# Fixing the order of the scan's output products: the two heads of a chunk in turn, then the products with the carried states

## The chip, the cores and the metric

The kernel runs on one core of one Trainium2 chip. The metric is the time of the whole program on the device in microseconds, lower is better. The time before the change is the median of three runs.

## What is computed

A decoder trunk of two layers on one sequence of 512 tokens, 1024 wide, all in float32. Layer 0 mixes by dilated attention, layer 1 by a Mamba-2 scan, and after each mixer stands a gated feed-forward part with a short convolution. The change lies in the scan of layer 1. Cut to that, the reference is:

```python
# 32 heads of 64, 8 groups of 4 heads, state 128, 4 chunks of 128 tokens
lmat   = jnp.exp(jnp.where(causal, seg, -jnp.inf))
cb     = jnp.einsum("bcign,bcjgn->bcijg", cm, bm)
y_diag = jnp.einsum("bcijgr,bcjgrp->bcigrp", cb[..., None] * lmat, xdt)
states = jnp.einsum("bcjgn,bcjgr,bcjgrp->bcgrpn", bm, decay, xdt)
# prev[c]: the state carried into chunk c, a recurrence over the chunks
y_off  = jnp.einsum("bcign,bcgrpn->bcigrp", cm, prev) * jnp.exp(a_cs)[..., None]
return (y_diag + y_off).reshape(b, s, h, p)
...
y = y + d_skip.astype(jnp.float32)[:, None] * xs
y = gated_group_rmsnorm(y.reshape(bsz, s, SSM_D_INNER), z, norm_w, SSM_GROUPS)
return y.astype(h.dtype) @ w_out
```

## The kernel before

Activations lie transposed, channels on the 128 partitions and 512 tokens along the free axis. Every large product is made of three products of rounded halves (high by high, low by high, high by low), each 128x128 by 128x512; all of them come from line 126 and fill one of three PSUM banks. A weight tile is loaded by SyncE's queue (line 113), rounded on ScalarE (line 117), and its low half is taken on VectorE, for the gate tiles z on GpSimd (line 118).

The scan goes through eight groups of four heads. `weave` sets the projections of the next group and products of the output matrix (tiles named wso) between the stages of `scan_group` for the present one, so that TensorE has long products to run while the small ones of the scan wait. A group has two halves x = 0 and 1 of two heads each; a half is called an output here, 16 in all, and 5.1 is group 5, x = 1. For an output:

- `by_token` turns x by tokens (px, line 648), scales it to `xdt` on VectorE (line 650) and to `xdd` on GpSimd (line 651).
- `states` makes three products `pst` (line 661), copies the first to `prev` on ScalarE (line 663), and adds the other two along the chunks on VectorE (lines 666 and 670). Chunks 1, 2 and 3 of the output need the first, second and third part of `prev`.
- `decays` loads a row of decays for each head, subtracts and takes the exponential, and multiplies by `cb` on GpSimd (line 688); the result is `lm`, one for each head.
- `outputs` is what is changed. `pf` are three products of the carried states with the C tile, 128 columns each and 128 rows of output (line 695). `py` are eight products, two heads by four chunks (line 702); each gives 64 rows of output, head 0 to the lower and head 1 to the upper 64 partitions of one bank, and so uses one half of the columns of the array. A float32 product stands in the trace as two records of TensorE: three pf are 6 records, eight py are 16. VectorE then joins py, pf, the skip term and the gate to `yt` (lines 708 to 713).

After both outputs of a group, `ss` (line 190) sums squares, `prg` (line 201) spreads the norm's factor, and VectorE and ScalarE make the two halves of y (lines 751 to 754), which the wso products read.

The order on each engine isn't the order of the code. A planner puts the instructions in order by times that it assumes, under the dependences; where a block stands under `tc.manual_schedule` for an engine, the instructions of the block keep the order of the code on that engine, and others may still come between them. An engine runs its instructions strictly in the planner's order, so an instruction that waits holds all behind it.

Of the kernel before, what the change touches and what calls it, by code (L numbers as in the profile page):

```python
# [14 lines left out]
P = 128  # L15
# [13 lines left out]
NCH = S // P  # L29
# [22 lines left out]
def trunk(ctx: ExitStack, tc: tile.TileContext, A, out):  # L52
    nc = tc.nc
    V, SC, G, T = nc.vector, nc.scalar, nc.gpsimd, nc.tensor
# [15 lines left out]
    def aux_bank(name):  # L70
        return ps.tile([P, 512], F32, tag="aux", name=name, bufs=3)

    def side_bank(name):
        return ps.tile([P, 512], F32, tag="side", name=name, bufs=2)

    def t2(name, tag, bufs, pool=k2, dtype=F32):
        return pool.tile([P, 512], dtype, tag=tag, name=name, bufs=bufs)

    def high_low(name):

        return t2(f"{name}h", "hl", 16, dtype=F32R), t2(f"{name}l", "hl", 16, dtype=F32R)
# [21 lines left out]
    def col(c):  # L103
        return par[:, c : c + 1]
# [79 lines left out]
    def inv_rms(ssum, n, r, more=None):  # L184

        p = aux_bank("ss")
        cn = r.shape[-1]
        for j in range(cn):
            js = slice(j * P, (j + 1) * P)
            T.matmul(p[:, j : j + 1], ssum[:, js], ones[:, 0:1], start=True, stop=more is None)  # L190
            if more is not None:
                T.matmul(p[:, j : j + 1], more[:, js], ones[:, 0:1], start=False, stop=True)
        ms = sm.tile([P, 4], F32, tag="ms", name="ms")
        V.tensor_scalar(ms[:, :cn], p[:, 0:cn], 1.0 / n, EPS, op0=ALU.mult, op1=ALU.add)
        G.tensor_tensor(r, ms[:, :cn], mhalf[:, :cn], op=ALU.pow)

    def along_free(r, name):

        p = aux_bank(name)
        for j in range(r.shape[-1]):  # L200
            T.matmul(  # L201
                p[:, j * P : (j + 1) * P], r[:, j : j + 1].to_broadcast([P, P]), ident,
                start=True, stop=True,
            )
        return p
# [342 lines left out]
    def b3(ap, n):  # L548

        return ap.unsqueeze(3).to_broadcast([ap.shape[0], ap.shape[1], ap.shape[2], n])  # L550
# [88 lines left out]
    def scan_group(g, d, ys):  # L639

        bt, ct, xs = d["b"], d["c"], (d["x0"], d["x1"])
        heads = [slice(4 * g + 2 * x, 4 * g + 2 * x + 2) for x in range(2)]
        xdt, xdd, prev, ee, lm = [], [], [], [], []

        def by_token(x):
            px = aux_bank("px")
            for c in range(NCH):
                T.transpose(px[:, c * P : (c + 1) * P], xs[x][:, c * P : (c + 1) * P], ident)
            t, u = t2("xdt", "xdt", 2, lp), t2("xdd", "tmp", 2, lp)
            V.tensor_tensor(v4(t), v4(px), b3(dt3[:, :, heads[x]], 64), op=ALU.mult)  # L650
            G.tensor_tensor(
                v4(u[:, 0:384], 3), v4(t[:, 0:384], 3), b3(dec3[:, 0:3, heads[x]], 64), op=ALU.mult
            )
            xdt.append(t)
            xdd.append(u)

        def states(x):
            pst = aux_bank("pst")
            for c in range(3):
                cs = slice(c * P, (c + 1) * P)  # L660
                T.matmul(pst[:, cs], btok[:, cs], xdd[x][:, cs], start=True, stop=True)
            t = t2("prev", "prev", 1, lp)
            SC.copy(t[:, 0:P], pst[:, 0:P])
            for c in range(1, 3):
                now, was = slice(c * P, (c + 1) * P), slice((c - 1) * P, c * P)
                V.tensor_tensor(
                    two(t[:, now]), two(t[:, was]),
                    cd3[:, c, heads[x]].unsqueeze(2).to_broadcast([P, 2, 64]), op=ALU.mult,
                )
                V.tensor_tensor(t[:, now], t[:, now], pst[:, now], op=ALU.add)  # L670
            prev.append(t)

        def decays(x):
            e_ = t2("ee", "ee", 2, lp)
            for hp in range(2):
                h = heads[x].start + hp
                t = t2("lm", "lm", 5, lp)
                dma(t, rows[h : h + 1, :].to_broadcast([P, S]))
                half = slice(hp * 64, (hp + 1) * 64)
                SC.activation(e_[half, P:512], t[half, P:512], AF.Exp)  # L680
                for c in range(NCH):
                    cs = slice(c * P, (c + 1) * P)
                    V.tensor_scalar(
                        t[:, cs], t[:, cs], acs[:, c * NSH + h : c * NSH + h + 1], 0.0,
                        op0=ALU.subtract, op1=ALU.min,
                    )
                SC.activation(t, t, AF.Exp)
                G.tensor_tensor(t, t, cb, op=ALU.mult)
                lm.append(t)
            ee.append(e_)  # L690

        def outputs(x):
            py, pf = side_bank("py"), side_bank("pf")
            for c in range(1, NCH):
                T.matmul(
                    pf[:, c * P : (c + 1) * P], prev[x][:, (c - 1) * P : c * P],
                    ct[:, c * P : (c + 1) * P], start=True, stop=True,
                )
            for hp in range(2):
                for c in range(NCH):  # L700
                    cs = slice(c * P, (c + 1) * P)
                    T.matmul(
                        py[hp * 64 : (hp + 1) * 64, cs],
                        xdt[x][:, c * P + hp * 64 : c * P + (hp + 1) * 64], lm[2 * x + hp][:, cs],
                        start=True, stop=True,
                    )
            yt = t2("yt", "yt", 2, lp)
            V.tensor_tensor(ee[x][:, P:512], ee[x][:, P:512], pf[:, P:512], op=ALU.mult)
            V.scalar_tensor_tensor(
                yt, xs[x], col(C_DSK + 2 * g + x), py, op0=ALU.mult, op1=ALU.add  # L710
            )
            V.tensor_tensor(yt[:, P:512], yt[:, P:512], ee[x][:, P:512], op=ALU.add)
            V.tensor_tensor(yt, yt, d[f"z{x}"], op=ALU.mult)
            sq = t2("gsq", "sq", 2)
            SC.activation(sq, yt, AF.Square)
            return yt, sq


        by_token(0)
        pb = aux_bank("pb")  # L720
        for c in range(3):
            T.transpose(pb[:, c * P : (c + 1) * P], bt[:, c * P : (c + 1) * P], ident)
        btok = t2("btok", "btok", 1, lp)
        SC.copy(btok[:, 0:384], pb[:, 0:384])
        pc = aux_bank("pc")
        for c in range(NCH):
            cs = slice(c * P, (c + 1) * P)
            T.matmul(pc[:, cs], bt[:, cs], ct[:, cs], start=True, stop=True)
        cb = t2("cb", "cb", 2, lp)
        V.tensor_tensor(  # L730
            cb.rearrange("p (c i) -> p c i", c=NCH), pc.rearrange("p (c i) -> p c i", c=NCH),
            tri.unsqueeze(1).to_broadcast([P, NCH, P]), op=ALU.mult,
        )
        yield
        decays(0)
        states(0)
        by_token(1)
        yield
        y0, sq0 = outputs(0)
        decays(1)  # L740
        states(1)
        yield
        y1, sq1 = outputs(1)
        V.tensor_tensor(sq0, sq0, sq1, op=ALU.add)
        yield
        rg = sm.tile([P, 4], F32, tag="rg", name="rg")
        inv_rms(sq0, 2 * P, rg)
        yield
        prg = along_free(rg, "prg")
        for x, y in enumerate((y0, y1)):  # L750
            V.scalar_tensor_tensor(y, y, col(C_GN + 2 * g + x), prg, op0=ALU.mult, op1=ALU.mult)
            y_h, y_l = high_low(f"y{g}{x}")
            SC.copy(y_h, y)
            V.tensor_tensor(y_l, y, y_h.bitcast(F32), op=ALU.subtract)
            ys.append((y_h, y_l))
# [181 lines left out]
```

## Time and profile before

| | |
|---|---|
| median of three runs | 1708.27 us (1706.97 to 1708.58) |
| the profiled execution, its own time | 1708.01 us |
| its span, first to last instruction | 1706.2 us |
| mean granted TensorE clock | 0.992 |
| TensorE products busy | 1675.4 us, 98% |
| VectorE, ScalarE, GpSimd busy | 64%, 40%, 28% |

The profile tells for each engine how long it was busy, how long it sat idle before an instruction, and which event ended that. Busy time of TensorE counts a product from its start to its modelled end, and neighbours overlap: two long products of 0.38 us follow at a distance of 0.22 us. So times on TensorE are read here from start to start. A full clock is 2.4 GHz and shows as 1.00, its other level 1.2 GHz as 0.50.

### The profile page before, as it was taken

Reading aid. Unit: us, or ns where it says so; the run is one execution under the profiler, and the core shown is the slowest. Engines: PE = TensorE matmul, PEld = TensorE weight load, DVE = VectorE, ACT = ScalarE, POOL = GpSimd, SP = SyncE. Lnnn points to the kernel's source line nnn. Section 1 sums busy time; section 2 is a strip of 40 time slices with the busy share of each in tenths; the row PEclk is TensorE's granted clock in tenths of the full one; section 3 lists DMA queues with packets and bytes.
Section 4 is the critical chain, followed back from the end, with each engine's and each line's share of the span. In section 5 each row is a group of like instructions: output and inputs, shape, how many; then the busy total and the mean of one; then the engine's idle time right before and its main releaser. Section 6 shows DMA issues by size and latency. Waiting matters only on the chain. (4 is left out here: it accounts for less than half of the span.)

```text
span 1706.2 us, 21506 instructions
## 1 busy us (share of the span) xinstructions
PE 1675.4 (98%) x8208; PEld 1414.4 (83%) x8208; DVE 1089.2 (64%) x1791; ACT 690.7 (40%) x1016; POOL 477.3 (28%) x312
## 2 busy tenths in 40 slices
PE   8999999999999999999999999999999999999997
PEld 6888888888888888888887888888887788888887
DVE  6366664366657746745568788787785774574565
ACT  4233332333344423423355655544562443343345
POOL 2344443144413211211242123322311321121024
PEclk9999999999999999999999999999999999999999
DMA  6222222222223223223133222232231222322324
GB/s 209 99 74 87 75 86 87 87 87 75 85 93 120 99 87 111 99 87 111 65 120 115 91 99 94 80 119 98 94 103 65 74 99 87 111 99 87 107 82 133
DMA packets 52342, 165.56 MB, mean 97 GB/s; under 512 B 5840, under 2 KB 8144, under 8 KB 52240
## 3 DMA queue, kind: packets, MB, share of 16 engines
q1 hardware_dynamic: 52240, 164.19, 28.9%
q8 instruction: 65, 1.06, 0.3%
q14 instruction: 37, 0.30, 0.1%
HBM read 162.01 MB, written 2.16 MB: 96 GB/s over the span
## 5 line engine op out<-in xcount | busy, mean ns | idle before, releaser
L126 PE MATMUL u<-xl,hi_u 128*128 128x512 f32 x704 | 271.3, 385 | 3.1 <-DVE xl L171 3.1
L126 PE MATMUL u<-xh,hi_u 128*128 128x512 f32 x704 | 271.2, 385 | 0.0
L126 PE MATMUL u<-xh,lo_u 128*128 128x512 f32 x704 | 271.0, 385 | 0.0
L517 POOL TENSOR_TENSOR au<-au,au 128x512 f32<-128x512 f32 x44 | 57.0, 1296 | 434.0 <-DVE au L497 413.3
L310 POOL TENSOR_TENSOR rotqk<-rotqk,sr 32x512 f32<-32x512 f32 x48 | 91.9, 1915 | 262.5 <-DVE rotqk L309 219.5
L497 DVE SCALAR_TENSOR_TENSOR au<-usu,par,au 128x511 f32<-128x511 f32 (+1 forms) x176 | 161.0, 919 | 6.8 <-ACT au L495 1.7
L117 ACT CAST hi_u<-raw_u 128x1024 fp32r<-128x1024 f32 x88 | 91.1, 1042 | 180.0 <-PE u L126 121.6
L126 PEld LDWEIGHTS u<-xl,hi_u 128*128 128x128 f32 x704 | 132.6, 188 | 29.8 <-DVE xl L171 4.6
L126 PEld LDWEIGHTS u<-xh,lo_u 128*128 128x128 f32 x704 | 132.5, 188 | 25.4
L126 PEld LDWEIGHTS u<-xh,hi_u 128*128 128x128 f32 x704 | 132.5, 188 | 25.3
L126 PE MATMUL qk<-xh,hi_qk 128*128 128x512 f32 x384 | 149.1, 388 | 0.0
L126 PE MATMUL qk<-xl,hi_qk 128*128 128x512 f32 x384 | 148.1, 386 | 0.0
L126 PE MATMUL qk<-xh,lo_qk 128*128 128x512 f32 x384 | 147.1, 383 | 0.0
L512 DVE TENSOR_TENSOR usu<-u,rbc 128x512 f32<-128x512 f32 x88 | 60.6, 691 | 118.1 <-PE u L126 111.6
L118 DVE TENSOR_TENSOR lo_u<-raw_u,hi_u 128x1024 fp32r<-128x1024 f32 x88 | 108.4, 1235 | 27.9 <-ACT hi_u L117 27.9
L530 DVE TENSOR_TENSOR xr<-xr,wd 128x512 f32<-128x512 f32 x40 | 27.2, 686 | 117.2 <-PE wd L126 117.2
L117 ACT CAST hi_qk<-raw_qk 128x1024 fp32r<-128x1024 f32 x48 | 50.2, 1046 | 127.9 <-PE qk L126 73.1
L117 ACT CAST hi_wd<-raw_wd 128x1024 fp32r<-128x1024 f32 (+1 forms) x56 | 52.5, 953 | 119.3 <-PE wd L126 74.7
L306 DVE TENSOR_TENSOR qk<-qk,cr 128x512 f32<-128x512 f32 x48 | 33.0, 687 | 91.0 <-PE qk L126 90.8
L182 POOL TENSOR_TENSOR ssum<-ssum,sq 128x512 f32<-128x512 f32 (+1 forms) x40 | 55.1, 1378 | 106.5 <-ACT sq L181 105.5
L126 PEld LDWEIGHTS qk<-xh,lo_qk 128*128 128x128 f32 x384 | 72.0, 188 | 13.2
L126 PEld LDWEIGHTS qk<-xh,hi_qk 128*128 128x128 f32 x384 | 72.1, 188 | 12.7
(631 smaller groups left out, 4052.0 us busy)
## 6 DMA issues: line engine op xcount, KB each, us to landing
raw_u<-in_wup SPq DMA_DIRECT2D x88, 512.0 KB, 3.2
raw_qk<-in_wqk SPq DMA_DIRECT2D x48, 512.0 KB, 3.2
raw_wd<-in_wdn SPq DMA_DIRECT2D x32, 512.0 KB, 3.2
raw_wd<-in_wdn SPq DMA_DIRECT2D x24, 384.0 KB, 2.9
raw_xs<-in_win SPq DMA_DIRECT2D x16, 512.0 KB, 3.2
raw_z<-in_win SPq DMA_DIRECT2D x16, 512.0 KB, 3.2
lm<-rows SPq DMA_DIRECT2D x32, 256.0 KB, 3.5
raw_wso<-in_wso SPq DMA_DIRECT2D x16, 512.0 KB, 3.3
```

Source lines behind the costliest of these rows:

```text
L117: SC.copy(hi[:, s], raw[:, s])
L118: low.tensor_tensor(lo[:, s], raw[:, s], hi.bitcast(F32)[:, s], op=ALU.subtract)
L126: T.matmul(in_turns(dst), w, in_turns(x), start=first, stop=last)
L182: G.tensor_tensor(ssum, ssum, sq, op=ALU.add)
L306: V.tensor_tensor(at(t), of(p), of(cr), op=ALU.mult)
L310: G.tensor_tensor(rot[R, :], rot[R, :], sr[R, :], op=ALU.mult)
L497: V.scalar_tensor_tensor(dst[:, j:], src[:, : S - j], col(c_w + taps - 1 - j), dst[:, j:], op0=ALU.mult, op1=ALU.add,)
L512: V.tensor_tensor(us, p, rbc, op=ALU.mult)
L517: G.tensor_tensor(ab[1], ab[0], ab[1], op=ALU.mult)
L530: V.tensor_tensor(xr[m], xr[m], p, op=ALU.add)
```

## The change

In `outputs`, the eight products py are put ahead of the three products pf. The heads alternate: for each chunk head 1, then head 0. The pf follow in one piece, last chunk first. The block stands under `manual_schedule` for TensorE, which keeps that order. No product is added or removed, and the other engines' work is the same.

```diff
--- before.py
+++ after.py
@@ -691,18 +691,21 @@
 
         def outputs(x):
             py, pf = side_bank("py"), side_bank("pf")
-            for c in range(1, NCH):
-                T.matmul(
-                    pf[:, c * P : (c + 1) * P], prev[x][:, (c - 1) * P : c * P],
-                    ct[:, c * P : (c + 1) * P], start=True, stop=True,
-                )
-            for hp in range(2):
+
+
+            with tc.manual_schedule(engines={mybir.EngineType.PE}):
                 for c in range(NCH):
                     cs = slice(c * P, (c + 1) * P)
+                    for hp in (1, 0):
+                        T.matmul(
+                            py[hp * 64 : (hp + 1) * 64, cs],
+                            xdt[x][:, c * P + hp * 64 : c * P + (hp + 1) * 64], lm[2 * x + hp][:, cs],
+                            start=True, stop=True,
+                        )
+                for c in reversed(range(1, NCH)):
                     T.matmul(
-                        py[hp * 64 : (hp + 1) * 64, cs],
-                        xdt[x][:, c * P + hp * 64 : c * P + (hp + 1) * 64], lm[2 * x + hp][:, cs],
-                        start=True, stop=True,
+                        pf[:, c * P : (c + 1) * P], prev[x][:, (c - 1) * P : c * P],
+                        ct[:, c * P : (c + 1) * P], start=True, stop=True,
                     )
             yt = t2("yt", "yt", 2, lp)
             V.tensor_tensor(ee[x][:, P:512], ee[x][:, P:512], pf[:, P:512], op=ALU.mult)
```

What the planner makes of it is seen on TensorE's order. In these rows a tile stands left of the arrow, what it is made from right of it; a number behind a name is that of the tile; [waits ...] names the engines waited for.

The first place is output 4.1 on TensorE, before:

```order
L126 MATMUL c_8913<-xl_97,hi_c_8908 128x4x32x4
L126 MATMUL c_8913<-xh_89,lo_c_8909 128x4x32x4
L695 MATMUL pf<-ac_8494,prev 128x128 [waits DVE_49,Activation_49]
L702 MATMUL py<-lm,xdt 64x128 [waits DVE_49]
L695 MATMUL pf<-ac_8494,prev 128x128 [waits DVE_49]
L702 MATMUL py<-lm,xdt 64x128 x6
L695 MATMUL pf<-ac_8494,prev 128x128 [waits DVE_49]
L702 MATMUL py<-lm,xdt 64x128
L126 MATMUL wso_8967<-y20h,hi_wso_8742 128x4x32x4
```

and now:

```order
L126 MATMUL c_8940<-xh_89,lo_c_8936 128x4x32x4
L700 MATMUL py<-lm,xdt 64x128 [waits DVE_49]
L700 MATMUL py<-lm,xdt 64x128 x7
L126 MATMUL wso_8997<-y20h,hi_wso_8766 128x4x32x4
L126 MATMUL wso_8997<-y20l,hi_wso_8766 128x4x32x4
L126 MATMUL wso_8997<-y20h,lo_wso_8767 128x4x32x4
L706 MATMUL pf<-ac_8515,prev 128x128 [waits DVE_49,PE_49]
L706 MATMUL pf<-ac_8515,prev 128x128
L706 MATMUL pf<-ac_8515,prev 128x128 [waits Activation_49]
L126 MATMUL wso_8997<-y21h,hi_wso_8766 128x4x32x4
```

The three pf stood between the py; now the eight py are one run and the three pf another, with three wso products between the runs, and the first pf waits for VectorE's last part of prev. Outputs 3.1 and 5.1 look the same.

The second place is output 0.0, the first of the scan, on TensorE before:

```order
L126 MATMUL xs_7285<-xh_82,lo_xs_7281 128x4x32x4
L695 MATMUL pf<-ac_6904,prev 128x128 [waits Activation_49]
L702 MATMUL py<-lm,xdt 64x128 [waits Pool_49]
L702 MATMUL py<-lm,xdt 64x128 [waits DVE_49] x2
L695 MATMUL pf<-ac_6904,prev 128x128 [waits DVE_49]
L702 MATMUL py<-lm,xdt 64x128
L702 MATMUL py<-lm,xdt 64x128 [waits Pool_49]
L702 MATMUL py<-lm,xdt 64x128
L695 MATMUL pf<-ac_6904,prev 128x128 [waits DVE_49]
L702 MATMUL py<-lm,xdt 64x128 x2
```

and now, 26 long products behind its eight py (which moved up by 18 long products):

```order
L126 MATMUL xs_7291<-xl_93,hi_xs_7286 128x4x32x4
L661 MATMUL pst<-xdd,btok 128x128 [waits PE_49,Pool_49]
L661 MATMUL pst<-xdd,btok 128x128
L706 MATMUL pf<-ac_6904,prev 128x128 [waits DVE_49]
L706 MATMUL pf<-ac_6904,prev 128x128
L706 MATMUL pf<-ac_6904,prev 128x128 [waits Activation_49]
L661 MATMUL pst<-xdd,btok 128x128
L700 MATMUL py<-lm,xdt 64x128 [waits PE_49]
```

The pf of output 0.0 now stand among the pst of output 0.1, and the last pst and the eight py of 0.1 are queued behind them.

The third place is the end of the scan on TensorE, where the last group's norm (prg) is followed by the products of its y (y70 and y71), before:

```order
L126 MATMUL wso_10302<-y61h,lo_wso_10241 128x4x32x4
L201 MATMUL prg<-ident,rg 128x128 [waits Pool_49]
L201 MATMUL prg<-ident,rg 128x128 x3
L126 MATMUL wso_10322<-y70h,hi_wso_10317 128x4x32x4 [waits Activation_49]
L126 MATMUL wso_10333<-y70h,hi_wso_10317 128x4x32x4 [waits DVE_49]
L126 MATMUL wso_10346<-y70h,hi_wso_10317 128x4x32x4 [waits DVE_49]
L126 MATMUL wso_10322<-y70l,hi_wso_10317 128x4x32x4 [waits DVE_49]
```

and now:

```order
L126 MATMUL wso_10350<-y51h,lo_wso_10283 128x4x32x4
L201 MATMUL prg<-ident,rg 128x128 [waits Pool_49]
L201 MATMUL prg<-ident,rg 128x128 x3
L126 MATMUL wso_10350<-y60h,hi_wso_10288 128x4x32x4
L126 MATMUL wso_10350<-y60l,hi_wso_10288 128x4x32x4
L126 MATMUL wso_10350<-y60h,lo_wso_10289 128x4x32x4
L126 MATMUL wso_10350<-y61h,hi_wso_10288 128x4x32x4
L126 MATMUL wso_10350<-y61l,hi_wso_10288 128x4x32x4
L126 MATMUL wso_10350<-y61h,lo_wso_10289 128x4x32x4
L126 MATMUL wso_10370<-y70h,hi_wso_10365 128x4x32x4 [waits Activation_49]
```

Six wso products of an older y, which stood ahead of prg, now stand behind it. In groups 1 to 7 the three pf of x = 0 follow their eight py directly, and the three pst of x = 1 come right behind them (in group 2 behind one long product more); in group 1, nine long products stood ahead of these pst before. GpSimd's order is unchanged.

## Rows read from the trace of the kernel before

**Rows 1.** The page's busy times by engine: us, share of the span, instructions.
```profile
PE 1675.4 (98%) x8208; PEld 1414.4 (83%) x8208; DVE 1089.2 (64%) x1791; ACT 690.7 (40%) x1016; POOL 477.3 (28%) x312
```

**Rows 2.** Three stretches: length, busy PE, PEld, DVE, ACT, POOL, then clock, DMA.
```profile
939.20:946.10 6.90, 6.42 (x24) 5.02 (x25) 6.30 (x14) 3.39 (x5) 0.00 (x0) 0.51 0.33 73
946.10:1307.80 361.70, 360.03 (x1917) 304.24 (x1916) 286.95 (x480) 188.61 (x257) 94.25 (x61) 1.00 0.29 94
...
1314.70:1321.50 6.80, 6.00 (x15) 4.73 (x15) 2.08 (x5) 0.16 (x1) 0.00 (x0) 0.50 0.23 80
```

**Rows 3.** TensorE's waits, 900 to 1320 us: total us, times, longest us.
```profile
PE pf L695 <- DVE prev L670: 3.1, 4, 2.1
PE wso L126 <- ACT y70h L753: 1.8, 1, 1.8
...
PE wso L126 <- DVE y70l L754: 0.8, 1, 0.8
PE pst L661 <- POOL xdd L651: 0.3, 1, 0.3
```

**Rows 4.** Groups by line, 944 to 1300 us: records, busy us, mean ns, idle.
```profile
L702 PE MATMUL py<-lm,xdt 128*64 128x128 f32 x240 | 28.0, 282 | 0.0
...
L695 PE MATMUL pf<-ac,prev 128*128 128x128 f32 x90 | 17.8, 294 | 1.1 <-DVE prev L670 1.0
```

**Rows 5.** Timeline of TensorE, output 3.0: start us, length us, records.
```profile
1083.15 0.83 PE L695 MATMUL pf<-ac,prev 128*128 128x128 f32 x6
1083.91 1.58 PE L702 MATMUL py<-lm,xdt 128*64 128x128 f32 x16
1085.42 0.94 PE L661 MATMUL pst<-xdd,btok 128*128 128x128 f32 x6
1086.11 0.47 PE L126 MATMUL c<-xh,hi_c 128*128 128x512 f32 x1
1086.43 0.39 PE L126 MATMUL c<-xl,hi_c 128*128 128x512 f32 x1
```

**Rows 6.** Timeline of TensorE, output 3.1.
```profile
1091.56 0.38 PE L695 MATMUL pf<-ac,prev 128*128 128x128 f32 x2
1091.88 0.43 PE L702 MATMUL py<-lm,xdt 128*64 128x128 f32 x2
1092.24 0.49 PE L695 MATMUL pf<-ac,prev 128*128 128x128 f32 x2
1092.66 1.15 PE L702 MATMUL py<-lm,xdt 128*64 128x128 f32 x12
...
1094.51 0.49 PE L126 MATMUL wso<-y00h,hi_wso 128*128 128x512 f32 x1
```

**Rows 7.** Timeline of TensorE, short runs of py in outputs 2.0 and 7.0.
```profile
1033.52 0.44 PE L702 MATMUL py<-lm,xdt 128*64 128x128 f32 x4
...
1282.05 1.09 PE L702 MATMUL py<-lm,xdt 128*64 128x128 f32 x8
```

**Rows 8.** Timeline of TensorE, long products and a py behind them.
```profile
986.72 0.39 PE L126 MATMUL xs<-xh,lo_xs 128*128 128x512 f32 x1
986.94 0.38 PE L126 MATMUL xs<-xh,hi_xs 128*128 128x512 f32 x1
987.26 0.32 PE L702 MATMUL py<-lm,xdt 128*64 128x128 f32 x1
```

**Rows 9.** Timelines of TensorE, GpSimd and VectorE, groups 0 and 1.
```profile
936.27 0.49 PE L695 MATMUL pf<-ac,prev 128*128 128x128 f32 x2 [0.98 <-ACT prev L663]
...
937.34 1.28 POOL L651 TENSOR_TENSOR xdd<-xdt,dec 128x384 f32<-128x384 f32 x1
...
940.52 0.29 DVE L670 TENSOR_TENSOR prev<-prev,pst 128x128 f32<-128x128 f32 x1
...
944.25 0.74 DVE L709 SCALAR_TENSOR_TENSOR yt<-axs,par,py 128x512 f32<-128x512 f32 x1
...
991.87 1.28 POOL L651 TENSOR_TENSOR xdd<-xdt,dec 128x384 f32<-128x384 f32 x1
```

## The prediction, made before the changed kernel ran

> **What bounds the kernel now.** I read the busy times first. TensorE is busy 98% of the span, the next engine 64% [rows 1]. Then the stretches of the scan: from 946 to 1308 us TensorE is busy 360.0 of 361.7 us at the full clock [rows 2]. So in the scan nearly every tenth of a microsecond taken from TensorE's instructions is taken from the program, as long as no other engine becomes late. Then the waits: in the scan TensorE stood idle for prev (3.1 us behind VectorE, 1.0 behind ScalarE), for the last group's y (1.8 and 0.8) and for xdd (0.3) [rows 3, 9]. Two stretches ran at the 1.2 GHz level, 939 to 946 and 1315 to 1321 us, each during or just after the longest of these waits [rows 2, 3, 9]. Last the timelines of single outputs, since the change is a matter of tenths [rows 5 to 7].
>
> **Term A, the products themselves.** The step is to find what alternating is worth. Two records of one head take 0.43 us and eight take 1.09: each further record adds 0.11, and four would take 0.65 [rows 6, 7]. But the four records at 1033.52 take only 0.44. They are the last product of head 0 and the first of head 1, which stand side by side in the order [rows 7]. So the two halves of the array work at once when products of both heads are at hand. In the order of before, one head's four chunks come ahead of the other's, and a whole run of 16 takes 1.58 [rows 5], partly overlapped. In the new order both streams should start together: eight records of one head, 1.09, and 0.01 for the other's lag, 1.10. That is 0.48 less.
>
> The second piece is the change between py and pf. From the last py to a pf pass 0.20 us (1091.88 + 0.43 - 0.27 to 1092.24, with 0.27 the length of a record, as the mean in [rows 4] has it), against 0.11 between neighbours; and a first pf behind py is late by another 0.11 (0.49 against 0.38 for two) [rows 6]. Before, output 3.1 changes kind five times and back to long products. It takes 2.95 from 1091.56 to 1094.51 [rows 6] plus 0.11 by which the next long product is late, 3.06. Afterwards: entry into py 0.10 (0.32 from the long product instead of 0.22 [rows 8]), the run 1.10 - 0.27 + 0.20 = 1.03, exit 0.11, together 1.24. The pf alone: six records, with pst as the row that is nearest in shape, take 0.69 behind py, less the 0.11 of the change of kind, plus 0.10 by which the next long product is late (0.32 instead of 0.22): 0.68 [rows 5, 8]. Sum 1.92, a gain of 1.14. Outputs 3.1, 4.1 and 5.1 are alike. In 3.0, 4.0 and 5.0 the pf stood in one piece ahead of the 16 [rows 5]; there the number of changes stays and only the 0.48 is gained.
>
> The other nine outputs from 0.1 on lie between these two shapes. In all, the fifteen have 28.0 + 17.8 = 45.8 us of py and pf [rows 4]. Three outputs like 3.0 take 3 x (0.83 + 1.58) = 7.2; three like 3.1 take 3 x (0.38 + 0.43 + 0.49 + 1.15 + 0.49 + 0.43) = 10.1 [rows 5, 6] (the second pf and the first py of rows 6 come once more at its end). That leaves 28.5, or 3.16 each, between 2.41 (gain 0.48) and 3.37 (gain 1.14). On the line between them that is 1.00 each. Term A for fifteen: 3 x 0.48 + 3 x 1.14 + 9 x 1.00 = 13.9. Output 0.0 has the shape of 3.1 and gets 1.1. **A = -15.0 us.**
>
> A rule of the Trainium skill speaks against the first step. The page TensorE: Matmul & The Clock Gate (Part 3, what overlaps and what doesn't) says that a load of weights overlaps a running product only where the two use different rows of the array; the two heads use all 128 rows and differ in columns. By it the 0.48 would not be gained, and the sum would lose 16 x 0.48. The trace doesn't agree: four records of both heads took 0.44.
>
> **Term B, the waits in the scan.** TensorE keeps its order, so what counts is when each input is ready at the new place. Before, waits for prev and xdd take 3.1 + 1.0 + 0.3 = 4.4 us [rows 3, 9].
>
> Output 0.0: its py now come 18 long products earlier and find lm made. The pf come 8 long products and one run of py later than before. Before, TensorE reached them at 935.3 (936.27 less the 0.98 that it waited [rows 9]); now it reaches the pst ahead of them at 935.3 + 8 x 0.22 + 1.2 = 938.3, waits for xdd, ready at 938.6 [rows 9], and reaches pf at 939.1. But the first pf now needs the last part of prev, ready at 940.8, and on VectorE one yt instruction (0.74) has come ahead of that part [rows 9]: 940.8 to 941.6. Wait 2.0 to 2.8, I take 2.4 with xdd's. Behind it on TensorE stand pst and py of output 0.1 and then the projection; nobody else is held for longer than that.
>
> Output 1.0: the waits for prev are covered, since 11 long products more stand ahead of the pf. But the three pst of 1.1 now follow at once, with nine long products less ahead of them. GpSimd makes their xdd at 991.87 + 1.28 = 993.15 [rows 9], behind the lm, in unchanged order. TensorE would be there at about 990.8 (992.9 before, less the 1.9 that output 1.0 gets shorter, waits included, and a long product). Wait 1.8 to 2.4: here the gain of output 1.0 is taken back. I take 2.1. For the rest I take 0.5: in groups 3 to 5 xdd and prev are ready some microseconds ahead. Sum 5.0 against 4.4. **B = +0.6** (bounds: -3.9 if all but 0.5 goes; +3.5 if each of these and the outputs of group 2 waits 0.5 to 1 more).
>
> **Term C, the end of the scan.** Prg to y of group 7 is a chain through VectorE and ScalarE in which TensorE idles 1.8 and 0.8 us [rows 3]. Six products of 0.22 now stand in it, 1.3 us of work for nothing; but VectorE gets one addition more ahead of the low half of y70, some 0.6. **C = -0.7** (bounds -1.3 and 0).
>
> **Term D, the clock.** In 939 to 946 TensorE was busy 6.4 of 6.9 us at the 1.2 GHz level, in 1315 to 1321 6.0 of 6.8 [rows 2]: half of that, 3.2 and 3.0 us, is lost. Before the first fall TensorE had waited 1.0 and 2.1 us within 5 us; the new waits at that place, 2.4 within 4 us, are much alike, so I keep the fall. The one at the end follows 1.8 and 0.8; the new wait is shorter, and it may stay at 2.4 GHz. The new wait in group 1 is as long as waits that were followed by a fall. **D = 0**, with -6.2 and +3.2 as ends.
>
> Sum: -15.0 + 0.6 - 0.7 = -15.1. The profiled execution took 1708.0 (1706.2 span and 1.8 around it), 0.3 from the median of 1708.27. 1708.0 - 15.1 = 1692.9, **1693 us**.
>
> **The rivals.**
> - The fixed order gives no overlap (the skill's rule above, as a mechanism: each load of weights waits for the other head's product). Then only the changes of kind are saved: A is 15.0 - 16 x 0.48 = 7.3, the time 1700.5. Against it the row of 0.44; for it, that this row is one pair, not eight in a row. Chance 0.07.
> - The slow stretches go. With pf behind py nothing holds TensorE long enough: one stretch gives 1690, both 1686.5, and without the wait of 0.0 some 1684. For it, the shorter waits at the end; against it, the 2.4 of output 0.0. Chance 0.22.
> - The waits move and grow. The piece of pf asks for the last part of prev first, so its two early products can't fill the wait. If four more outputs wait 2.1 us, as the longest wait for prev now, and one slow stretch of 3.2 comes with them, 11.6 go: 1704.5. For it, the four waits behind VectorE in [rows 3]; against it, that three of them come to 1.0 us, and that the py now stand ahead as cover. Chance 0.13.
> - Slower: the same mechanism everywhere. If each of 16 pieces stood 2.1 us, 33.6 less the 5.0 in B would be added: about 1721. It decides against the kernel from a mean wait of about 1.3 us for each output (15.1 + 5.0 over 16). Against it: after the first output TensorE was idle only 1.7 of 361.7 us [rows 2]. Chance 0.04.
> - The change doesn't do what it says, or the gain is taken back by y, lm or the weights later on: TensorE arrives earlier and waits there. VectorE was busy 287 of 361.7 us [rows 2], so it has room. Time 1706 to 1710, chance 0.04.
>
> **How the numbers follow.** The forecast has 0.50, with 1689 to 1697 as its own range. The range reaches over the first two rivals and half of the third: 1683 to 1701. A difference of 0.2%, 3.4 us, is about what a measurement can tell from none. Faster by more: 0.50 + 0.07 + 0.22 + 0.13 = 0.92; within it 0.04; slower 0.04.
>
> **What would show it.** Right: runs of 16 py of about 1.10 us; 16 records and 6 records in one run each; py busy near 17.6 us for 16 outputs (28.0 for 15 before); a wait of pf for prev near 941 us and one of pst for xdd in group 1; TensorE still above 98%. Wrong: runs of 16 that still take 1.5 us (term A); waits of pf for prev in groups 3 to 5, or a third stretch at 0.50 (B and D); new waits of the long products for halves of weights or of y, which would mean that another engine had become the bound.

## The result and the profile after

The changed kernel took 1695.24 us (median of four runs, 1691.93 to 1698.64), the kernel before 1707.9 beside it: a ratio of 0.9927, 95% interval 0.9914 to 0.9941. That is 12.7 us less where 15.1 were forecast, 2.2 us above the forecast of 1693 and inside the range. On a second occasion (run `again`, below) the ratio was 0.9922 [0.9909, 0.9936]. The profiled execution took 1691.93 us (span 1690.1), the lowest of the four and 16.1 below the 1708.01 of the profile before.

Busy times by engine, as in [rows 1]:

```profile
PE 1658.2 (98%) x8208; PEld 1399.0 (83%) x8208; DVE 1085.5 (64%) x1791; ACT 690.1 (41%) x1016; POOL 478.8 (28%) x312
```

TensorE still sets the time; its busy time fell by 17.2 us with the same number of records, the others did as much as before.

The groups of py and pf over all 16 outputs, 917 to 1320 us (records, busy us, mean ns, idle ahead of them):

```profile
L700 PE MATMUL py<-lm,xdt 128*64 128x128 f32 x256 | 17.5, 279 | 0.0
L706 PE MATMUL pf<-ac,prev 128*128 128x128 f32 x96 | 14.1, 283 | 2.1 <-DVE prev L670 2.1
```

These answer [rows 4], which covers 15 outputs: 17.5 is 16 times 1.09. The timeline of TensorE at output 3.1 (start, length), which answers [rows 6]:

```profile
1084.20 0.38 PE L126 MATMUL wso<-y00h,lo_wso 128*128 128x512 f32 x1
1084.51 1.09 PE L700 MATMUL py<-lm,xdt 128*64 128x128 f32 x16
1085.53 0.49 PE L126 MATMUL wso<-y01h,hi_wso 128*128 128x512 f32 x1
...
1089.20 0.38 PE L126 MATMUL xs<-xl,hi_xs 128*128 128x512 f32 x1
1089.42 0.83 PE L706 MATMUL pf<-ac,prev 128*128 128x128 f32 x6
```

Sixteen records take 1.09 us where they took 1.58 [rows 5]. The way into py costs 0.31 instead of 0.22, as before. The six pf among long products enter at the usual 0.22.

TensorE's waits in the same stretch as [rows 3], 900 to 1320 us (us in total, times, longest):

```profile
PE ss L190 <- DVE gsq L747: 2.3, 2, 1.5
PE pf L706 <- DVE prev L670: 2.1, 1, 2.1
PE prg L201 <- POOL rg L195: 1.9, 2, 1.7
PE u L126 <- DVE xl L171: 1.7, 2, 1.2
PE pst L661 <- POOL xdd L651: 1.1, 2, 0.6
PE wso L126 <- DVE xr L775: 1.0, 1, 1.0
PE wso L126 <- ACT y70h L756: 0.2, 1, 0.2
```

Pf waits once instead of five times. The waits of the norm have grown: ss, the sum of squares, waits for VectorE's gsq, and prg for GpSimd's rg. Before, ss waited 0.2 us and prg not long enough to be listed; a wait for xr lay at 1328 us, still in the scan (the kernel before, 900 to 1330 us):

```profile
PE wso L126 <- DVE xr L772: 0.6, 1, 0.6
...
PE ss L190 <- DVE gsq L744: 0.2, 1, 0.2
```

(The waits of u belong to the feed-forward behind the scan; before they lay beyond 1330 us.)

Stretches of the changed kernel, with the columns of [rows 2]:

```profile
939.20:946.10 6.90, 4.76 (x36) 4.09 (x37) 6.65 (x14) 2.43 (x4) 0.00 (x0) 1.00 0.34 113
...
1253.80:1257.20 3.40, 3.40 (x9) 2.72 (x10) 3.02 (x5) 3.37 (x5) 0.30 (x1) 0.50 0.02 5
...
1318.60:1325.40 6.80, 4.44 (x10) 3.08 (x11) 4.36 (x3) 0.05 (x1) 3.07 (x2) 0.50 0.22 77
```

The stretch at 939 ran at the full clock this time, though TensorE was busy only 4.76 of its 6.90 us; a new one at 1.2 GHz begins within a microsecond of the longer of the two waits of ss (1.5), and the one at 1318 lies in the feed-forward, which begins at 1312.7. None is left at the end of the scan, where one of 6.8 us lay before [rows 2].

**An account of the scan.** To compare kernels I took TensorE's records from the first px of the scan to the first product of the feed-forward behind it. For each record the distance to the next start is what it costs; from that, time in which the engine waited is put apart, and of what ran at 1.2 GHz one half counts as lost. What py and pf add to a stream of long products, the ways in and out included, is "own"; the late start of the second long product behind them, some 0.09 to 0.10 us each, is not in it. Own, waits, lost and a remainder make up the length; the remainder was 353.3 to 357.3 us, so the first three columns carry most of the differences, but not all: it is the same within 0.3 us in two executions of one kernel (355.9 and 355.6 for the changed one, 354.4 and 354.5 for pf_asc), and 353.7 before. All figures are us of the one profiled execution of each; medians and ratios are of the timed runs.

| kernel | own | waits | lost at 1.2 GHz | scan | median | ratio to before |
|---|---|---|---|---|---|---|
| before | 43.7 | 8.0 | 6.3 | 411.7 | 1706.6 to 1708.9 | 1 |
| the changed kernel | 29.0 | 8.7 | 1.7 | 395.3 | 1695.24 | 0.9927 |
| again (the same) | 28.8 | 8.6 | 6.6 | 399.6 | 1695.59 | 0.9922 |
| alt_only | 34.5 | 9.7 | 3.3 | 402.2 | 1702.01 | 0.9964 |
| piece_only | 38.2 | 4.6 | 1.5 | 399.0 | 1694.49 | 0.9919 |
| pf_asc | 29.4 | 6.4 | 1.6 | 391.8 | 1689.31 | 0.9886 |
| asc_again (the same) | 29.4 | 6.5 | 1.7 | 392.1 | 1689.71 | 0.9895 |
| heads_asc | 38.4 | 6.6 | 0.0 | 400.8 | 1697.76 | 0.9950 |
| asc_pairs | 30.3 | 6.8 | 1.8 | 392.7 | 1691.38 | 0.9903 |
| alt_late | 30.0 | 6.5 | 0.0 | 391.0 | 1688.09 | 0.9888 |
| pf_first | 26.7 | 8.5 | 0.0 | 392.5 | 1691.55 | 0.9906 |
| after_sqv | 29.0 | 14.1 | 7.7 | 405.7 | 1702.38 | 0.9978 |
| piece_sqv | 37.5 | 5.5 | 0.0 | 396.3 | 1696.12 | 0.9940 |
| asc_sqv | 29.9 | 7.6 | 1.7 | 392.7 | 1690.95 | 0.9909 |

The intervals of the ratios are 0.0008 to 0.0017 to either side. The theory with which I went in was that of the prediction: alternating saves some 8 us and fewer ways in and out of py some 7, on TensorE's own time, and little is given back. The rivals were that waits or the clock decide.

### The profile page after: what moved, and what is told of

It is laid out like the page before. It is cut to its first block, busy times and chain, and to the rows that moved or that the text cites. A ratio compares the mean times of both kernels' runs of the same rounds, so it can differ in the third digit from the quotient of the medians.

```text
span 1690.1 us, 21485 instructions
## 1 busy us (share of the span) xinstructions
PE 1658.2 (98%) x8208; PEld 1399.0 (83%) x8208; DVE 1085.5 (64%) x1791; ACT 690.1 (41%) x1016; POOL 478.8 (28%) x312
## 5 line engine op out<-in xcount | busy, mean ns | idle before, releaser
L118 DVE TENSOR_TENSOR lo_u<-raw_u,hi_u 128x1024 fp32r<-128x1024 f32 x88 | 110.0, 1254 | 26.9 <-ACT hi_u L117 26.9
## 6 DMA issues: line engine op xcount, KB each, us to landing
raw_wd<-in_wdn SPq DMA_DIRECT2D x24, 384.0 KB, 3.0
```

What stands on the lines that cost most here:

```text
L118: low.tensor_tensor(lo[:, s], raw[:, s], hi.bitcast(F32)[:, s], op=ALU.subtract)
```

## The experiments

### The same again, and each half of the change alone

`again` is the changed kernel once more.

> The changed kernel once more, to see what its four times from 1691.9 to 1698.6 us are made of. Theory: the products save the same in every run (two heads' runs of 1.09 us, 31 us of TensorE for py and pf in all), and the spread is in the number of stretches at the 1.2 GHz level, about 3 us each; so the times go with the granted clock, 0.995 near 1692 to 1694 and 0.991 near 1697 to 1699, and a profile at 0.991 shows one or two stretches more than the first profile, behind one of the waits of 1.5 us or more. Rival: the waits themselves (for prev, for the sum of squares, for the norm's factor) differ from run to run; then the idle time before TensorE's instructions in the scan, 8.6 us in the first profile, differs by several us at the same clock.

It took 1695.59 us (1691.97 to 1697.1). Its profiled execution took 1697.1, which can be set beside the 1691.93 of the first. Its waits in the scan were the same within 0.2 us, but it had these stretches at 1.2 GHz, besides those at 1259 and 1324 us that answer to the two of the first (columns as above):

```profile
941.50:948.30 6.80, 6.04 (x29) 5.11 (x30) 6.55 (x14) 3.57 (x6) 0.00 (x0) 0.50 0.29 100
...
1306.70:1310.10 3.40, 3.40 (x10) 2.63 (x9) 1.05 (x2) 0.00 (x0) 0.00 (x0) 0.51 0.64 231
...
494.40:497.80 3.40, 3.40 (x10) 2.63 (x9) 2.38 (x3) 2.98 (x4) 0.00 (x0) 0.50 0.08 12
```

One half of 6.8 + 3.4 + 3.4 is 6.8 us against the 5.2 by which the two spans differ. So the spread between these two executions of one kernel comes from which places fall to the lower clock, not from the waits. That is the theory, but with three stretches more and not one or two; the one at 494 lies far from anything that was changed, behind a wait of 2.1 us which both executions have.

`alt_only` alternates the heads and leaves the pf ahead of them in the code, in the planner's hands:

```diff
+            for c in range(1, NCH):
+                T.matmul(pf ...)
             with tc.manual_schedule(engines={mybir.EngineType.PE}):
                 for c in range(NCH):
                     for hp in (1, 0):
...
-                for c in reversed(range(1, NCH)):
-                    T.matmul(pf ...)
```

> The heads alternate in a fixed order, the three products with the carried states are left to the planner, as before. Theory: unbroken runs of 16 records take 1.09 us, and the pieces of pf still break up most outputs, so that only some 5 to 7 us of the products' 15 are gained: 1701 to 1703 us, with the wait for prev in the first output back as before. Rival (the gain lies in the piece of pf and the waits that it moves, not in the overlap): about 1707. Rival (the overlap is nearly all of it): 1695 or less.

It took 1702.01 us (1699.91 to 1703.43), as the theory had it. Own fell by 9.2, which is less than the 14.7 of the whole change since the pf still cut the runs of py; the waits rose by 1.7.

`piece_only` fixes the order, py first and then the pf reversed, but takes head 0's four chunks and then head 1's:

```diff
-                for c in range(NCH):
-                    for hp in (1, 0):
+                for hp in (0, 1):
+                    for c in range(NCH):
```

> The three products with the carried states follow in one piece, last chunk first, but the four chunks of head 0 stand ahead of those of head 1. Theory: runs of 16 take 1.58 us as before, each output costs TensorE about 0.48 us more than in the changed kernel, 7.7 us in 16 outputs: 1700 to 1704 us; the planner puts half of an output's products elsewhere in four places, which costs some tenths each. Rival (no overlap is gained by alternating): the same as the changed kernel, 1695. Rival (the piece itself brings nothing): 1707.

This missed: 1694.49 us (1691.7 to 1695.6), no slower than the changed kernel. The theory was right on TensorE and wrong on the time. Its py do take what they should:

```profile
L700 PE MATMUL py<-lm,xdt 128*64 128x128 f32 x256 | 27.1, 279 | 0.1
```

That is 9.6 us more busy than in the changed kernel, and own is 9.2 more. But its waits are 4.1 us less. TensorE's waits in `piece_only`, 900 to 1320 us:

```profile
PE wso L126 <- ACT y70h L756: 1.9, 1, 1.9
PE pf L706 <- DVE prev L670: 1.3, 1, 1.3
PE wso L126 <- DVE y70l L757: 0.8, 1, 0.8
PE ss L190 <- DVE gsq L747: 0.5, 1, 0.5
```

Against the changed kernel's list, ss waits 1.8 us less and prg not at all. One profile against one, scan against scan, it is 3.7 us longer (399.0 and 395.3); by the medians nothing is left. So either alternating is worth little in time whatever surrounds it, or this pair hides its worth. The next runs were made to tell which.

`pf_asc` is the changed kernel with the pf in ascending order, so that the first two needn't wait for the last part of prev:

```diff
-                for c in reversed(range(1, NCH)):
+                for c in range(1, NCH):
```

> As the changed kernel, with the three products with the carried states in ascending order of chunks. The planner then sets them apart in most outputs, so that each waits only for its own part of prev. Theory: TensorE waits less for prev in the first output (2.1 us in the changed kernel), but each pf set apart costs 0.1 to 0.25 us more for its change of kind, some 20 of them: 1695 to 1698, the same or slightly slower. Rival (the wait for the last part of prev and what it brings is the main loss): 1690 or less.

This missed on the good side: 1689.31 us (1685.96 to 1690.06), in the same set of runs as the 1695.59 of the changed kernel; the intervals of the two ratios don't touch. Own is the same within 0.6 us. The waits are 2.3 less; its list, 900 to 1320 us:

```profile
PE pf L706 <- ACT prev L663: 2.4, 1, 2.4
PE pst L661 <- POOL xdd L651: 1.0, 1, 1.0
PE pf L706 <- DVE prev L670: 0.9, 1, 0.9
...
PE ss L190 <- DVE gsq L747: 0.6, 1, 0.6
PE prg L201 <- POOL rg L195: 0.6, 1, 0.6
```

The wait of output 0.0 is about as long as in the changed kernel (2.4; there 2.6 with xdd's); it only stands ahead of another pf, and a later output now waits 0.9 for prev. What is gone is most of ss and prg, 4.2 us down to 1.2. So the rival's time came, but not by a shorter wait for prev. With the order of the pf the planner's order changes on VectorE and ScalarE too, and not on GpSimd; that the waits of the norm fall is shown, the step by which they do is not. Of the 3.5 us by which the scans of the two profiles differ, 2.3 are waits and 1.5 the remainder; the medians differ by more, since the changed kernel's first profile was its fastest execution.

### What alternating is worth where the waits are alike

`heads_asc` is pf_asc with the heads one after the other; with pf_asc it makes the same pair as piece_only and the changed kernel.

> As pf_asc (py first, the three pf in one piece, ascending), but head 0's four chunks come ahead of head 1's. It asks what alternating is worth where the pf are ascending. Theory (alternating saves 9 us of TensorE's own time and in pf_asc the waits leave most of it): py cost 25 to 26 us of TensorE against 16.5, some 1 to 4 us less waiting, so 1694 to 1698. Rival (what alternating saves is always taken back, as piece_only and the changed kernel seemed to say): within 1.5 us of pf_asc, 1688 to 1691.

1697.76 us (1697.24 to 1698.61), at the upper end of the theory: 8.1 to 8.5 above the two medians of pf_asc, 9 to 11 by the ratios to the kernel before (0.9950 against 0.9895 and 0.9886). Own is 9.0 more, the waits are alike (6.6 and 6.4); the 1 to 4 us less of waiting that the theory allowed didn't come. So in this pair nearly all of what alternating saves on TensorE arrives in the time, and the rival falls. That in the other pair it didn't, the table puts down to the waits there (8.7 against 4.6) and to the stretches at the lower clock (1.7 and 6.6 lost in the two executions of the changed kernel, 1.5 in piece_only).

### Taking a step out of the norm's chain

If the waits of ss and prg take the gain back, shortening the chain ahead of them should return it. In the kernels so far ScalarE makes the square, and it stands there in a queue with loads of tables of 1.28 us. Three kernels make it on VectorE:

```diff
-            SC.activation(sq, yt, AF.Square)
+            V.tensor_tensor(sq, yt, yt, op=ALU.mult)
```

> The changed kernel with the square of yt on VectorE instead of ScalarE. In the changed kernel ss stands 2.25 us and prg 1.9 us; the square waits on ScalarE behind loads of tables of 1.28 us and behind ee. Theory (the norm's chain takes back a part of what alternating saves): the waits of ss fall below 0.5 us, the time by 2 to 4 us, 1691 to 1694. Rival (these waits only stand in for others, such as those of weights or pf): the sum of waits stays near 9 us, 1695 to 1697. If VectorE, with 16 instructions of 0.69 us more, becomes the bound: over 1697.

> piece_only (heads one after the other, the pf in one reversed piece) with the square of yt on VectorE. In piece_only ss stands 0.5 us and prg not at all, since TensorE comes later. Theory (the chain matters only where the products are short): no gain, 1693.5 to 1696. Rival (the square on VectorE is simply the better place, whatever the products): 2 to 4 us less, 1690.5 to 1692.5.

> pf_asc with the square of yt on VectorE. In pf_asc ss stands 0.6 us and prg 0.6 us. Theory: those 1.2 us are all there is to gain, 1687.5 to 1689.5. Rival (square on VectorE better everywhere): 1685 to 1687. If VectorE becomes late: over 1690.

`after_sqv` took 1702.38 us (1699.84 to 1705.66; its profile is of the slowest): no gain but 7 us lost, over the 1697 that was given for a VectorE that becomes the bound, with own unchanged at 29.0. `piece_sqv` took 1696.12 (1693.83 to 1698.76), no gain, just above the theory's range. `asc_sqv` took 1690.95 (1689.83 to 1691.91), no gain either, in the range that was given for a late VectorE. The edit did not do what it was for: ss in after_sqv waits more, not less. Its list:

```profile
PE wso L126 <- DVE xr L775: 4.3, 1, 4.3
PE ss L190 <- DVE gsq L747: 3.3, 3, 1.7
PE pf L706 <- DVE prev L670: 3.3, 3, 2.1
...
PE prg L201 <- POOL rg L195: 1.3, 2, 1.1
```

The longest of these can be followed through three engines. Timelines of TensorE, VectorE and ScalarE around it (the brackets give the idle time and what ended it):

```profile
1268.43 0.79 PE L126 MATMUL wso<-y40h,hi_wso 128*128 128x512 f32 x1 [4.26 <-DVE xr L775]
```

```profile
1266.56 1.23 DVE L118 TENSOR_TENSOR lo_wso<-raw_wso,hi_wso 128x1024 fp32r<-128x1024 f32 x1 [4.33 <-ACT hi_wso L117]
1267.70 1.28 DVE L775 TENSOR_TENSOR xr<-xr,wso 128x512 f32<-128x512 f32 x2
```

```profile
1261.72 1.28 ACT L617 ACT_TABLE_LOAD   x1
1263.02 0.63 ACT L617 ACTIVATE usz<-usz 128x512 f32<-128x512 f32 x1
1263.66 1.28 ACT L687 ACT_TABLE_LOAD   x1
1264.96 0.63 ACT L687 ACTIVATE lm<-lm 128x512 f32<-128x512 f32 x1
1265.49 1.03 ACT L117 CAST hi_wso<-raw_wso 128x1024 fp32r<-128x1024 f32 x1
```

TensorE needs the bank that VectorE's xr empties; xr stands behind a low half of weights, which waits for ScalarE's rounding, and that stands behind lm and z taken in turn, each with a load of tables. With the square gone from ScalarE the planner's order has 46 such loads in the whole program instead of 40. So this run doesn't tell whether the norm's chain takes the gain back. It tells that 14.1 us of waits and 7.7 lost at the lower clock can stand beside the same own time.

### How the two heads share the array, and where the pf belong

`asc_pairs` alternates by two chunks instead of one:

```diff
-                for c in range(NCH):
-                    for hp in (1, 0):
+                for c0 in (0, 2):
+                    for hp in (1, 0):
+                        for c in (c0, c0 + 1):
```

> As pf_asc, but the heads alternate by two chunks: head 1's chunks 0 and 1, head 0's chunks 0 and 1, then chunks 2 and 3. A run of 16 records took 1.58 us with the heads one after the other and 1.09 with the heads in turn; eight records of one head alone took 1.09, so 16 of one head would take some 2.0. Theory (TensorE begins records some way ahead of those that still wait for their half of the array, four or so as 2.0 less 1.58 says): the run takes 1.09 to 1.20, py cost 16.5 to 18.5 us, the time within 2 us of pf_asc, 1688 to 1691. Rival (only two products that are neighbours in the order share the array, 0.23 saved at each of the three changes of head): the run takes 1.34, py cost some 20.5 us, the time 1692 to 1695.

One run of 16 in each of the two kernels, first asc_pairs, then heads_asc:

```profile
1076.35 1.15 PE L701 MATMUL py<-lm,xdt 128*64 128x128 f32 x16
```

```profile
1088.18 1.58 PE L700 MATMUL py<-lm,xdt 128*64 128x128 f32 x16
```

1.15 us, own 30.3: the theory holds and the rival's 1.34 doesn't. The time, 1691.38 (1689.48 to 1692.21), is 0.4 above the range that the theory gave. So a record can begin while several in front of it wait for their half of the array. The single starts in the trace say the same: in the run of heads_asc above, records begin at 0, 160, 269, 378, 488, 493, 597, 653, 706, 763, 815 and 872 ns and further on, and the record that signals the end of head 0 is the one at 815. Those at 493, 653 and 763 are thus of head 1 and began ahead of head 0's last. What was said of the kernel before, that an engine runs its instructions strictly in the planner's order, doesn't hold for the starts of two heads' products.

`alt_late` fixes the alternating py alone and writes the pf behind them, ascending, for the planner to place:

```diff
-                for c in reversed(range(1, NCH)):
-                    T.matmul(pf ...)
+            for c in range(1, NCH):
+                T.matmul(pf ...)
```

> As pf_asc, but only the alternating py are fixed; the pf stand behind them in the code in ascending order and the planner places them. It puts TensorE's instructions in nearly the same order as in pf_asc. Theory (what counts is that the pf come behind py and that the early ones needn't wait for the last part of prev, not that the piece is fixed): 1687 to 1692. Rival (the gain of pf_asc over the changed kernel was an accident of its place on VectorE and ScalarE, which differ a little here): 1693 to 1697.

1688.09 us (1687.84 to 1689.66), as the theory had it. By the names of the tiles the order on TensorE, VectorE, ScalarE and GpSimd is that of pf_asc throughout; fixing the piece adds nothing, since the planner sets it so by itself.

`pf_first` fixes the three pf, ascending, ahead of the alternating py; the planner then sets nearly every pf apart among long products:

```diff
             with tc.manual_schedule(engines={mybir.EngineType.PE}):
+                for c in range(1, NCH):
+                    T.matmul(pf ...)
                 for c in range(NCH):
                     for hp in (1, 0):
...
-                for c in reversed(range(1, NCH)):
-                    T.matmul(pf ...)
```

> The heads alternate in a fixed run of eight py, and the three pf are fixed ahead of it, ascending; the planner sets nearly every pf apart among long products. Theory (each pf set apart costs changes of kind, and TensorE meets prev earlier): py 16.5 us, pf and the long products behind them 3 to 6 us more than in pf_asc, waits for prev 1 to 3 us more, so 1693 to 1698. Rival (only the alternation counts, the place of the pf doesn't): 1688 to 1691.

1691.55 us (1689.5 to 1693.97): neither's range, between the two. The waits are 2.1 more than in pf_asc (8.5), but not those that the theory named: for prev they are 2.5 us against 3.3. It is pst that waits longer for xdd, 3.0 instead of 1.0, and the end of the scan, 1.5 for y70h. Its list, 900 to 1320 us:

```profile
PE pst L661 <- POOL xdd L651: 3.0, 2, 1.6
PE pf L698 <- DVE prev L670: 1.6, 1, 1.6
PE wso L126 <- ACT y70h L756: 1.5, 1, 1.5
```

The theory's cost on TensorE didn't come either. Own is 26.7, the lowest of all, but the remainder is the highest, 357.3; together they are 384.0 against 383.8 in pf_asc, so a pf set apart costs no more and no less. The rows show why. A pf between long products of pf_first, and the run of py:

```profile
1075.21 0.39 PE L126 MATMUL c<-xl,hi_c 128*128 128x512 f32 x1
1075.43 0.38 PE L698 MATMUL pf<-ac,prev 128*128 128x128 f32 x2
1075.57 0.47 PE L126 MATMUL c<-xh,lo_c 128*128 128x512 f32 x1
1075.88 0.39 PE L126 MATMUL c<-xh,hi_c 128*128 128x512 f32 x1
...
1079.45 0.38 PE L698 MATMUL pf<-ac,prev 128*128 128x128 f32 x2
1079.76 1.09 PE L705 MATMUL py<-lm,xdt 128*64 128x128 f32 x16
```

A pf follows a long product at the usual 0.22, the next long one comes 0.14 behind its first record, and the one after that 0.31 later instead of 0.22. That is 0.23 for a pf set apart, about the two times 0.11 that it takes in a piece. The slow way in (from the last record of pf to py pass 0.20) and the slow way out are py's alone; the late start of the second long product stands behind pf as behind py, and lies in the remainder.

`asc_again` is pf_asc on another occasion.

> pf_asc once more on another occasion. It took 1689.3 us, a ratio of 0.9886. If the ascending order is what makes it better than the changed kernel: ratio 0.987 to 0.991, 1686 to 1691. If that was one good chip or one lucky set of runs: ratio 0.992 to 0.994.

1689.71 us (1689.51 to 1689.8), ratio 0.9895 (0.9880 to 0.9910), in the range for an ascending order that is better; its interval just touches that of `again` (0.9909 to 0.9936), and lies below that of the changed kernel's first set. pf_asc, on both occasions, and alt_late beat both kernels, by 18 to 20 us against the kernel before and, by the medians, 5.5 to 7.5 against the changed one.

## Why the prediction was right

- **What bounds the kernel**: right. TensorE stayed at 98%, and own, waits and lost together explain the length of every kernel's scan to within the 4.0 us by which the remainders differ.
- **Term A, -15.0**: the change of own is 29.0 - 43.7 = -14.7. By outputs: 3.1, 4.1 and 5.1 gained 1.26, 1.25 and 1.25 (said: 1.14, but with the late start of the long product behind, which own leaves out; with it they gained 1.16, 1.16 and 1.15), 3.0, 4.0 and 5.0 gained 0.38 or 0.39 (0.48), the nine others 8.7 together (9.0), and 0.0 gained 1.16 (1.1). The pair of records in [rows 7] was enough to foretell 1.09 for a full run. The words "change of kind" were too wide, as pf_first showed: only ways into and out of py cost, and a pf set apart among long products costs nothing. In the order that was predicted this made no difference, since nearly every pf that stood apart before had py for a neighbour. The page TensorE: Matmul & The Clock Gate of the Trainium skill (Part 3, what overlaps and what doesn't) lets a load of weights overlap only where the rows of the array differ, and says that products start strictly in the order of the program. All runs of 16 here speak against the first, 1.09 us for two heads that use the same rows, and the starts of heads_asc against the second.
- **Term B, +0.6**: the place was right, the list was not. Output 0.0 waited 0.47 for xdd and 2.14 for prev, 2.6 against 2.4; the rows are

```profile
938.49 0.71 PE L661 MATMUL pst<-xdd,btok 128*128 128x128 f32 x4 [0.47 <-POOL xdd L651]
941.34 0.94 PE L706 MATMUL pf<-ac,prev 128*128 128x128 f32 x6 [2.14 <-DVE prev L670]
```

  The wait of group 1 was 0.65 instead of 2.1 (0.47 in `again`). There I had set a GpSimd that keeps its time against a TensorE that comes sooner. But GpSimd's lm wait for VectorE's cb, cb needs TensorE's pc, and all of it came sooner: cb began at 978.50 instead of 985.08, xdd at 985.32 instead of 991.87 [rows 9], while TensorE reached pst at 986.0, where I had 990.8. Timeline of GpSimd in the changed kernel:

```profile
979.26 6.09 POOL L688 TENSOR_TENSOR lm<-lm,cb 128x512 f32<-128x512 f32 x4 [3.46 <-DVE cb L733]
985.32 1.27 POOL L651 TENSOR_TENSOR xdd<-xdt,dec 128x384 f32<-128x384 f32 x1
```

  And the waits of the norm, ss and prg, 4.2 us, were in no term. Before they were 0.2 for ss and too short to be listed for prg, so the rows of waits gave no warning; that the long products between an output and its ss are the only cover they have could have been read from the order. In all, waits for prev, xdd, gsq and rg rose from 4.7 to 7.4: +2.7 instead of +0.6. This is the term that was mis-sized most.
- **Term C, -0.7**: the waits at the end of the scan fell from 3.2 (1.8, 0.8 and the 0.6 for xr at 1328 us, which the term left out) to 1.2, -2.0, beyond its bound of -1.3; the longer of the two that are left is one for VectorE's xr.
- **Term D, 0**: this differs from one execution to the next. The loss in the scan was 6.3 before, 1.7 in the first profile after and 6.6 in the second. The first, with -4.6, goes far to explain why it took 1691.93; the second, with +0.3, took 1697.1, and had the third stretch in the scan that the prediction named as a sign against it.
- **The sum**: by the table, own -14.7, waits +0.7, lost -4.6 and the remainder +2.2 make the -16.4 by which the scan of the first profile is shorter. For `again` they are -14.9, +0.6, +0.3 and +1.9, together -12.1. The medians of two occasions say -12.7 and -13.3, between the two. The forecast of -15.1 was right in mechanism and about 2 us too good. The waits as a whole are only 0.8 of that (+0.7 instead of -0.1): that term C gave back 1.3 more than was said, and so covered most of the 2.1 that term B missed, was luck. The larger part is the remainder, which no term held. Of its 2.2 us, 1.8 are long products between long products: with what ran at 1.2 GHz counted half, they stand 225.0 ns from start to start on the mean instead of 223.6 (224.6 in `again`), some 1265 of them. What slowed them no run tells.
- **The rivals**: no overlap is refuted by every run of 16. The slow stretches going is what happened in part in some executions. Waits that grow happened, but with 2.7 us, and at the norm rather than at prev. Nothing was slower; after_sqv shows how the slower end could have come about, by 14.1 us of waits, and even that stayed below the kernel before.
- **What the prediction did not see**: it priced alternating and the piece as parts that add up. alt_only kept 9.2 of own and 6.9 us of time, piece_only 5.5 of own and 14 us of time, both together 14.7 and 13. The time of one part can't be read from a kernel that has it alone, since each new order lays all engines out anew, and the waits between kernels that compute the same ranged from 4.6 to 14.1 us. Why the reversed pf are harmless with the heads one after the other (piece_only is 3 us below heads_asc by the medians, 5 by the ratios) and cost 6 with alternating heads stays open.

## What to carry to other kernels

Where two small products use different halves of the array, set them near each other in the order; by twos was nearly as good as in turn (1.15 and 1.09 us against 1.58), and it is worth all it saves on TensorE only where other engines keep pace. Keep products that use half of the array in one run, since here each way in or out cost about 0.1 us; the full-width products set apart among long ones cost nothing here (0.23 against 0.22), and asking first for the input that is ready first was worth some 6 us with the heads in turn, though 3 to 5 us the other way with one head after the other. When a planner lays out the other engines anew, price the chain behind the moved step too (here the norm), and compare several orders before crediting one edit with a difference of a few microseconds.

## What the runs showed of the hardware

- Two heads' records begin 6 to 7 ns apart when they stand in turn, and 13 to 14 ns apart with two chunks of each; in both cases a pair of streams took hardly longer than one stream of eight, 1.09 [rows 7].
- With the heads one after the other, three records of the second began ahead of the first's last one, which is why 16 records took 1.58 and not twice 1.09.
- Behind a small product, of half or of full width, the second long product starts late: 0.30 to 0.33 us behind the first on the mean instead of 0.22, in every kernel traced.
- The same kernel with the same waits fell to 1.2 GHz at 1254 and 1319 us in one execution, and at 494, 941, 1259, 1307 and 1324 us in the next (leaving out the last microseconds of the program); 939 to 946 us ran at 2.4 GHz with TensorE busy 4.76 of 6.90 us in the one, and 941 to 948 at 1.2 GHz in the other.
